# Expert stage: five row tiles instead of three between a turning and its eviction, and tokens turned one run ahead

## The chip, the cores and the metric

The kernel runs on one core of a Trainium2 chip. The metric is device time in microseconds, the median over several runs. A profile of one further execution gives the rows below; its times are microseconds from the start of the span unless marked ns. PE is TensorE, PEld its weight load, DVE VectorE, ACT ScalarE, POOL GpSimd, SP SyncE; L878 is line 878 of the kernel.

## The reference, cut to what matters

Two transformer blocks over 512 tokens of width 1024 in float32. The first has, after a mixing layer, 32 experts of which each token takes 4. The rest (retention, pooling, attention with an index, the projections) lies before and behind the stage that is changed.

```python
top_vals, top_idx = lax.top_k(logits, TOP_K)
gates = jax.nn.softmax(top_vals, axis=-1)
...
gu = lax.ragged_dot(xs, w_gu, group_sizes) + b_gu[sorted_e]
gate = jnp.minimum(gu[:, ::2], SWIGLU_LIMIT)
up = jnp.clip(gu[:, 1::2], -SWIGLU_LIMIT, SWIGLU_LIMIT)
act = (up + 1.0) * (gate * jax.nn.sigmoid(SWIGLU_ALPHA * gate))
y = lax.ragged_dot(act.astype(w_down.dtype), w_down, group_sizes) + b_down[sorted_e]
y = y * gates.reshape(-1)[order][:, None].astype(y.dtype)
out = jnp.zeros_like(xt).at[tok].add(y.astype(xt.dtype))
```

## The kernel before, in words

**Precision.** A float32 product is made of products of two parts: ScalarE copies a float32 tile to a rounded one, the high part (L877, wh), and VectorE subtracts it from the original, the low part (L878, wl). Both are needed before TensorE can finish a tile.

**Experts.** The experts are sorted by load. Wide ones have 96 slots (`CAP`), narrow ones 64 (`FEW`); `LESS[e]` says which: 0 and 1 are wide, from 2 on narrow and wide alternate, and the last, 31, is narrow too. For a wide tile TensorE makes three products for each half of 512 columns (L165 to L167), six in all. For a narrow one, high and low part of the tokens lie side by side as one stationary operand of 128 columns, so four products do (L882); the two halves of the result are then added by a "fold".

**Runs of row tiles.** Each expert has three runs of eight row tiles: `gate_up(e, 0)`, `gate_up(e, 1)` and `down(e)`. A row tile is 128 rows of a weight matrix by 1024 columns. The order is gate_up(e, 0), down(e - 1), gate_up(e, 1), and so on, so wide and narrow runs alternate. `chunks` loads two tiles by one DMA of 1024 KB on SP's queue (L145, buffers wr), splits each, multiplies, and calls `next_tile()`.

**Work between the tiles.** `later([(d, fn), ...])` hands in small steps, and `next_tile` emits a step once d more tiles have been emitted. The steps are:

- `turned` (L846): transposes the gathered tokens of the next expert, four and four (`begin`, L205), and evicts each four as a high part on ScalarE (L216) and a low part on VectorE (L217) (`end`, by `split_in`).
- `clamped` (L915), for a half of a wide expert: clamp on VectorE (L910, L911), gelu on ScalarE (L912), mul on VectorE (L913), four transposes on TensorE (L205), eviction by `split_in` to the activations a.
- `folded` (L925), for a half of a narrow one: a copy gs on ScalarE (L939), the fold on TensorE (L938), clamp, gelu, mul, and `split_in`.
- `scatter` (L943): a scaled copy ys on ScalarE (L948), and an indirect DMA on POOL's queue that adds the rows to y_d (L950).
- `table` makes the slot indices of the next experts, `gather` fetches their tokens (L837, POOL's queue), and `gated_bias` (L1027), once behind expert 10, makes the gated bias of the down-projections.

**What sets the order.** The framework orders the instructions of each engine itself, from the order in which they are emitted and from what it takes to be ready at a time; each engine then runs its own list strictly in order. PSUM tiles: three pairs of banks for products (mm), two banks for transposes and folds (tr). The split parts stand in a ring of six tiles, so ScalarE and VectorE can be at most six tiles ahead of TensorE.

Of the kernel before, what the change touches and what calls it, by code (L numbers as in the profile page):

```python
# [9 lines left out]
F32 = mybir.dt.float32  # L10
# [4 lines left out]
AF = mybir.ActivationFunctionType  # L15
ALU = mybir.AluOpType
# [4 lines left out]
NE = 32  # L21
TOPK = 4
CAP = 96
# [3 lines left out]
FEW = 64  # L27
LESS = [i >= 2 and (i % 2 == 0 or i == 31) for i in range(NE)]
NT = 4
# [91 lines left out]
class Kern:  # L121
# [10 lines left out]
    def next(self, ring):  # L132

        ring.append(ring.pop(0))
        return ring[-1]
# [75 lines left out]
        for j in range(2):  # L211
            self.split_in(self.transpose4(src, 4 * j, m=m, pool=pool), dst[j], sl)

    def split_in(self, ps, dst, sl):
        dh, dl = dst
        self.nc.scalar.activation(dh[:, :, sl], ps, AF.Copy)  # L216
        self.nc.vector.tensor_tensor(out=dl[:, :, sl], in0=ps, in1=dh[:, :, sl].bitcast(F32), op=ALU.subtract)  # L217

    def halves(self, pool, name):

# [562 lines left out]
    def moe(self, f, Q):  # L783
        tc, nc, I, c = self.tc, self.nc, self.I, self.c
        self.psum(f, "m", 3, 2)
        P = f.enter_context(tc.tile_pool(name="mp", bufs=1))
        T = f.enter_context(tc.tile_pool(name="mt", bufs=2))
# [14 lines left out]
        tabs = {}  # L802
        X = {}
        halves = [[self.wh[0].tile([128, 2, 1024], F32R, tag=tag, name=tag) for tag in ("wh", "wl")] for _ in range(2)]
        parts = [[a[:, i] for a in pair] for i in range(2) for pair in halves]
# [4 lines left out]
        def later(stages):  # L810

            self.late += [(self.at_tile + d, fn) for d, fn in stages]
# [12 lines left out]
        def tables(e, t3):  # L825
            for j in range(BATCHES[e]):
                tabs[e + j] = [a[:, j:j + 1] for a in t3]

        def table(e):

            ps = self.mm.tile([128, 2, 512], F32, tag="mm", name="mm")
            gen = self.slots_by(e, BATCHES[e], Q, ps[:, 0, :])
            later([(j, lambda: next(gen)) for j in range(BATCHES[e])] + [(BATCHES[e] + 2, lambda: tables(e, next(gen)))])
# [7 lines left out]
        def pair(m, tag):  # L841

            t = T.tile([128, 8, 2 * m], F32R, tag=tag, name=tag)
            return t[:, :, 0:m], t[:, :, m:2 * m], t

        def turned(x, m):  # L846

            p = pair(m, "x2")
            tp = {}

            def begin(j):
                tp[j] = self.transpose4(x, 4 * j, m=m)

            def end(j):
                self.split_in(tp[j], [a[:, 4 * j:4 * j + 4] for a in p[0:2]], slice(0, m))
            return p, [(1, lambda: begin(0)), (3, lambda: begin(1)), (4, lambda: end(0)), (6, lambda: end(1))]

        def turn(e):
            X[e], stages = turned(xgs[e % 2], FEW if LESS[e] else CAP)
            return stages  # L860
# [54 lines left out]
        def clamped(ps, half, p):  # L915

            gu = ps.rearrange("p a (m s) -> p (a m) s", s=2)
            gt, up = (T.tile([CAP, 512], F32, tag=tag, name=tag) for tag in ("ag", "au"))
            clamp, gelu, mul = glu(gt, up)
            tp = []  # L920
            return [(3, lambda: clamp(gu[:, :, 0], gu[:, :, 1])), (5, gelu), (6, mul),
                    (7, lambda: tp.append(self.transpose4(up, m=CAP))),
                    (10, lambda: self.split_in(tp[0], [a[:, 4 * half:4 * half + 4] for a in p[0:2]], slice(0, CAP)))]

        def folded(ps, half, p):  # L925


            gs = T.tile([128, 2, 512], F32, tag="gs", name="gs")
            v = gs.rearrange("p a (m s) -> p (a m) s", s=2)
            gt, up = (T.tile([128, 4, FEW], F32, tag=tag, name=tag) for tag in ("ag", "au"))  # L930
            clamp, gelu, mul = glu(gt, up)
            tp = []

            def fold():
                tp.append(self.tr.tile([128, 8, FEW], F32, tag="tr", name="tr"))
                for s in range(2):
                    for b in range(4):
                        nc.tensor.matmul(tp[0][:, 4 * s + b, :], v[:, b * 128:b * 128 + 128, s], c["fold"], start=True, stop=True)  # L938
            return [(3, lambda: nc.scalar.activation(gs, ps, AF.Copy)), (4, fold), (6, lambda: clamp(tp[0][:, 0:4], tp[0][:, 4:8])),  # L939
                    (7, gelu), (8, mul),  # L940
                    (9, lambda: self.split_in(up, [a[:, 4 * half:4 * half + 4] for a in p[0:2]], slice(0, FEW)))]

        def scatter(ps, gate, rows, n=1):  # L943

            self.n += 1
            m = ps.shape[0]
            y = ys[0:m, self.n % 2, :]
            nc.scalar.activation(y, ps.rearrange("p a n -> p (a n)"), AF.Copy, scale=gate[0:m])  # L948
            for o in range(0, m, m // n):
                nc.gpsimd.indirect_dma_start(out=self.y_d[:, :], out_offset=bass.IndirectOffsetOnAxis(ap=rows[0:m // n], axis=0),  # L950
                                             in_=y[o:o + m // n], in_offset=None, bounds_check=S - 1, oob_is_err=False,
                                             compute_op=ALU.add)
# [11 lines left out]
        def gate_up(e, half, raw=()):  # L964
            m = 128 if LESS[e] else CAP
            ps = self.mm.tile([m, 2, 512], F32, tag="mm", name="mm")

            def bias(n, first):
                r = FEW if LESS[e] else CAP
                nc.tensor.matmul(ps[0:r, n, :], sel[:, e:e + 1].to_broadcast([128, r]),  # L970
                                 bt[:, half * 1024 + n * 512:half * 1024 + n * 512 + 512], start=first, stop=False)
            ex = expert(e)
            chunks(lambda r, n: wgu[ex, r:r + n, half * 1024:half * 1024 + 1024], ps, X[e], raw, bias, LESS[e])
            if half == 0:
                A[e] = pair(FEW if LESS[e] else CAP, "a2")
            later((folded if LESS[e] else clamped)(ps, half, A[e]))

        def down(e):
            ps = self.mm.tile([128 if LESS[e] else CAP, 2, 512], F32, tag="mm", name="mm")
            ex = expert(e)  # L980
            chunks(lambda r, n: wdn[ex, r:r + n, :], ps, A[e], few=LESS[e])
            later([(3, lambda: scatter(ps, tabs[e][1], tabs[e][0], 2 if LESS[e] else 1))])

        def overflow():

# [41 lines left out]
        def gated_bias():  # L1027

            bd = T.tile([128, D], F32, tag="gs", name="bd")
            for r in range(0, 128, NE):  # L1030
                nc.sync.dma_start(bd[r:r + NE], I["expert_b_down"][0])
            g4 = T.tile([128, NT, 4, NE], F32, tag="ag", name="g4")
            nc.vector.tensor_copy(g4, self.G[:, :, None, :].to_broadcast([128, NT, 4, NE]))
            gT = P.tile([128, S], F32R, name="gT")
            bs = P.tile([128, D], F32R, name="bs")
            tp = self.tr.tile([128, 512], F32, tag="tr", name="tr")
            for t in range(NT):
                nc.tensor.transpose(tp[:, self.tok(t)], g4[:, t].rearrange("p a e -> p (a e)"), c["ident"])

            def parts():  # L1040
                nc.scalar.activation(gT, tp, AF.Copy)
                for r in (32, 96):
                    q = slice(r, r + NE)
                    nc.vector.tensor_tensor(out=gT[q], in0=tp[q], in1=gT[q].bitcast(F32), op=ALU.subtract)
                nc.scalar.activation(bs, bd, AF.Copy)
                nc.vector.tensor_tensor(out=bs[64:128], in0=bd[64:128], in1=bs[64:128].bitcast(F32), op=ALU.subtract)

            def products(t):
                ps = self.mm.tile([128, 2, 512], F32, tag="mm", name="mm")
                for n in range(2):  # L1050
                    nc.tensor.matmul(ps[:, n, :], gT[:, self.tok(t)], bs[:, n * 512:n * 512 + 512], start=True, stop=True)
                later([(3, lambda: nc.scalar.activation(self.h[:, t, :], ps.rearrange("p a n -> p (a n)"), AF.Copy))])
            later([(3, parts)] + [(4 + 8 * t, lambda t=t: products(t)) for t in range(NT)])

        ne = self.ne
        self.gates(self.G[:, :, 0:2], self.tcols0, 2, T)
# [18 lines left out]
        for e in range(ne):  # L1075
            if e == 0:
                table(2)
            gate_up(e, 0, raws)
            if e + 2 < ne:
                gather(e + 2)  # L1080
            if 0 < e < ne - 1:
                down(e - 1)
            if e + 1 < ne:
                later(turn(e + 1))
            if e + 3 in BATCHES:
                table(e + 3)
            gate_up(e, 1, raws)
            if e == min(10, ne - 1):
                gated_bias()
# [483 lines left out]
```

## Time and profile before

| what | us |
|---|---|
| median of 3 runs | 1867.5 |
| lowest, highest | 1863.9, 1867.83 |
| the profiled execution: its time | 1864.25 |
| the profiled execution: its span | 1862.5 |
| PE busy | 1762.6 (95%) |
| DVE busy | 1535.5 (82%) |
| ACT busy | 1186.7 (64%) |

The span goes from the first to the last instruction. Matmuls are pipelined and their ends are modelled, so a full PE is not PE at its peak. The expert stage fills the span from about 236 to 1394 us (first and last L878). "DMA share" is the mean busy share of the sixteen DMA engines.

### The profile page before, as it was taken

What the parts mean: (1) busy time and instruction counts of PE and PEld (TensorE: products, weight loads), DVE (VectorE), ACT (ScalarE), POOL (GpSimd) and SP (SyncE); (2) the same over time, 40 slices, a digit from 0 to 9 for tenths busy, and PEclk for the clock granted to TensorE, in tenths of its full rate; (3) what the DMA queues carried; (4) which work ended last, traced back from release to release, by engine and by line L of the source; (5) the groups of instructions that cost most, each with busy time, mean ns of one, the idle gap of its engine ahead of it and who ended that gap; (6) DMA issues with size and microseconds to landing.
All of it is one profiled execution on the core that took longest, in us unless ns stands there. A gap on an engine that the chain in (4) does not pass through costs nothing.

```text
span 1862.5 us, 24800 instructions
## 1 busy us (share of the span) xinstructions
PE 1762.6 (95%) x8378; PEld 1278.2 (69%) x8379; DVE 1535.5 (82%) x2637; ACT 1186.7 (64%) x1584; POOL 188.2 (10%) x120
## 2 busy tenths in 40 slices
PE   8999779899999899999999999999998999999999
PEld 6887547666666566666666666666666877787776
DVE  5574479799999789999999999999987869999542
ACT  5224258677778777777877777877875545564431
POOL 0011210121111011311110210210100000000000
PEclk9999879999999899999999999999998999999999
DMA  8225568999999999999999999999986222211211
GB/s 282 89 85 170 164 208 314 335 367 373 361 381 375 337 340 380 336 387 386 370 388 389 344 381 386 372 383 389 361 310 217 91 66 64 91 46 46 85 57 40
DMA packets 147625, 491.10 MB, mean 264 GB/s; under 512 B 14273, under 2 KB 18625, under 8 KB 147424
## 3 DMA queue, kind: packets, MB, share of 16 engines
q1 hardware_dynamic: 137600, 462.02, 66.5%
q0 software_dynamic: 8064, 22.68, 5.3%
q10 hardware_dynamic: 1824, 4.72, 0.7%
q8 instruction: 68, 1.11, 0.2%
q14 instruction: 69, 0.57, 0.1%
HBM read 470.90 MB, written 23.07 MB: 265 GB/s over the span
## 4 chain that ended last, share of the span: by engine, by line
PE 37%; DVE 18%; ACT 4%; issue 4%; DMA 1%; SPq 0%; ACTq 0%; DVEq 0%
DVE wl L878 9%; PE mm L167 8%; PE mm L166 8%; PE mm L165 8%; PE mm L882 5%; ACT wh L877 3%; PE tr L938 2%; PE tr L205 2%; PE po L1389 2%; PE tr L1472 1%; DVE isc L1335 1%; PE tr L1445 1%; DVE wl L159 1%; DVE au L913 1%; DVE m L1334 1%
## 5 line engine op out<-in xcount | busy, mean ns | idle before, releaser
L878 DVE TENSOR_TENSOR wl<-wr,wh 128x1024 fp32r<-128x1024 f32 x762 | 889.3, 1217 | 31.8 <-ACT wh L877 31.0
L877 ACT ACTIVATE wh<-wr 128x1024 fp32r<-128x1024 f32 x762 | 747.0, 1049 | 23.9 <-PE mm L166 11.2
L167 PE MATMUL mm<-wl,x 128*96 128x512 f32 x512 | 207.7, 406 | 6.2 <-DVE wl L878 5.7
L882 PE MATMUL mm<-wl,x 128*128 128x512 f32 x512 | 180.8, 434 | 28.2 <-DVE wl L878 28.0
L165 PE MATMUL mm<-wh,x 128*96 128x512 f32 x512 | 204.8, 400 | 2.5 <-ACT wh L877 2.1
L166 PE MATMUL mm<-wh,x 128*96 128x512 f32 x512 | 203.6, 398 | 0.0
L882 PE MATMUL mm<-wh,x 128*128 128x512 f32 x512 | 166.8, 397 | 0.1
L882 PEld LDWEIGHTS mm<-wl,x 128*128 128x128 f32 x512 | 81.6, 189 | 98.9 <-DVE wl L878 91.1
L950 POOL DMA_INDIRECT y_d<-ys,gi x48 | 97.8, 2037 | 438.0 <-ACT ys L948 260.4
L167 PEld LDWEIGHTS mm<-wl,x 128*96 128x96 f32 x512 | 83.5, 163 | 53.9 <-DVE wl L878 22.1
L837 POOL DMA_INDIRECT xg<-hn_d,gi x32 | 59.0, 1844 | 591.2 <-PE tr L205 540.7
L165 PE MATMUL mm<-wh,x2h 128*128 128x512 f32 (+2 forms) x288 | 115.6, 401 | 3.2 <-ACT x2h L216 3.2
L882 PEld LDWEIGHTS mm<-wh,x 128*128 128x128 f32 x512 | 96.1, 189 | 26.0 <-ACT wh L877 0.7
L166 PE MATMUL mm<-wh,x2l 128*128 128x512 f32 (+2 forms) x288 | 112.5, 391 | 0.5 <-DVE x2l L217 0.5
L167 PE MATMUL mm<-wl,x2h 128*128 128x512 f32 (+2 forms) x288 | 112.0, 390 | 0.1
L159 DVE TENSOR_TENSOR wl<-wr,wh 128x2048 fp32r<-128x2048 f32 (+3 forms) x40 | 76.4, 1915 | 38.5 <-ACT wh L158 38.3
L166 PEld LDWEIGHTS mm<-wh,x 128*96 128x96 f32 x512 | 83.8, 164 | 34.2 <-DVE x L217 0.4
L165 PEld LDWEIGHTS mm<-wh,x 128*96 128x96 f32 x512 | 83.8, 164 | 33.4 <-ACT wh L877 3.0
L167 PE MATMUL mm<-wl,a 128*96 128x512 f32 x256 | 104.4, 408 | 1.9 <-DVE wl L878 1.8
L165 PE MATMUL mm<-wh,a 128*96 128x512 f32 x256 | 101.4, 396 | 0.0
L166 PE MATMUL mm<-wh,a 128*96 128x512 f32 x256 | 101.1, 395 | 0.0
L912 ACT ACTIVATE ag<-ag 96x512 f32<-96x512 f32 (+1 forms) x64 | 33.6, 525 | 100.9 <-DVE ag L910 100.8
(438 smaller groups left out, 3134.6 us busy)
## 6 DMA issues: line engine op xcount, KB each, us to landing
wr<-in_expert_w_gate_up_dram SPq DMA_DIRECT2D x253, 1024.0 KB, 8.4
wr<-in_expert_w_down_dram SPq DMA_DIRECT2D x128, 1024.0 KB, 9.3
wr<-in_w_in_dram SPq DMA_DIRECT2D x20, 1024.0 KB, 5.0
wr<-in_w_out_dram SPq DMA_DIRECT2D x8, 1024.0 KB, 4.9
wr<-in_ple_gate_w_dram SPq DMA_DIRECT2D x4, 1024.0 KB, 9.0
wr<-in_w_in_dram SPq DMA_DIRECT2D x4, 512.0 KB, 6.9
xt<-in_x_dram POOLq DMA_DIRECT2D x8, 256.0 KB, 5.4
y_d<-h ACTq DMA_DIRECT2D x4, 512.0 KB, 3.0
```

The costliest lines, as they stand in the source:

```text
L159: nc.vector.tensor_tensor(out=lo[:, sl], in0=raw[:, sl], in1=hi[:, sl].bitcast(F32), op=ALU.subtract)
L165: mm(out, a[0], b[0], start=first, stop=False)
L166: mm(out, a[1], b[0], start=False, stop=False)
L167: mm(out, a[0], b[1], start=False, stop=last)
L205: self.nc.tensor.transpose(ps[:, j, :], src[0:m, (i0 + j) * 128:(i0 + j + 1) * 128], self.c["ident"][0:m, 0:m])
L837: nc.gpsimd.indirect_dma_start(out=xgs[e % 2][0:m], out_offset=None, in_=self.hn_d[:, :], in_offset=bass.IndirectOffsetOnAxis(ap=tabs[e][0 ...
L877: nc.scalar.activation(hi, w[:, kk], AF.Copy)
L878: nc.vector.tensor_tensor(out=lo, in0=w[:, kk], in1=hi.bitcast(F32), op=ALU.subtract)
L882: nc.tensor.matmul(ps[:, n, :], pair[2][:, k, :], part[:, n * 512:n * 512 + 512], start=k == 0 and part is hi, stop=k == 7 and part is lo)
L938: nc.tensor.matmul(tp[0][:, 4 * s + b, :], v[:, b * 128:b * 128 + 128, s], c["fold"], start=True, stop=True)
L950: nc.gpsimd.indirect_dma_start(out=self.y_d[:, :], out_offset=bass.IndirectOffsetOnAxis(ap=rows[0:m // n], axis=0), in_=y[o:o + m // n], i ...
L1389: nc.tensor.matmul(po[:, hd, :], pt[:, a * (i + 1) + k, :], v[:, k, vcol(hd)], start=(k == 0), stop=(k == i))
```

## The change

`split_in` takes a letter for the high or the low part, so that the two can be handed in as steps of their own, one tile apart. The places of the steps, in tiles behind the end of the run (or the call):

| step | before | after |
|---|---|---|
| tokens, first four: turn; high, low | 1; 4, 4 | 1; 6, 7 |
| tokens, last four: turn; high, low | 3; 6, 6 | 8; 13, 14 |
| wide half: transposes; high, low | 7; 10, 10 | 6; 11, 12 |
| narrow half: gs copy, fold, clamp, gelu, mul; high, low | 3, 4, 6, 7, 8; 9, 9 | 4, 5, 8, 9, 10; 11, 12 |
| scatter | 3 | 4 |
| gated_bias: parts, products | 3, 4 + 8t | 5, 6 + 8t |

The tokens of expert e + 1 are handed in ahead of down(e - 1) instead of behind it, thus eight tiles sooner. The gates of `gated_bias` are spread by four small copies in tiles of their own instead of one copy in a tile that the gelu's input shares.

```diff
-    def split_in(self, ps, dst, sl):
+    def split_in(self, ps, dst, sl, which="hl"):
         dh, dl = dst
-        self.nc.scalar.activation(dh[:, :, sl], ps, AF.Copy)
-        self.nc.vector.tensor_tensor(out=dl[:, :, sl], in0=ps, in1=dh[:, :, sl].bitcast(F32), op=ALU.subtract)
+        if "h" in which:
+            self.nc.scalar.activation(dh[:, :, sl], ps, AF.Copy)
+        if "l" in which:
+            self.nc.vector.tensor_tensor(out=dl[:, :, sl], in0=ps, in1=dh[:, :, sl].bitcast(F32), op=ALU.subtract)
...
-            def end(j):
-                self.split_in(tp[j], [a[:, 4 * j:4 * j + 4] for a in p[0:2]], slice(0, m))
-            return p, [(1, lambda: begin(0)), (3, lambda: begin(1)), (4, lambda: end(0)), (6, lambda: end(1))]
+            def end(j, which):
+                self.split_in(tp[j], [a[:, 4 * j:4 * j + 4] for a in p[0:2]], slice(0, m), which)
+            return p, [(1, lambda: begin(0)), (6, lambda: end(0, "h")), (7, lambda: end(0, "l")),
+                       (8, lambda: begin(1)), (13, lambda: end(1, "h")), (14, lambda: end(1, "l"))]
...
-                    (7, lambda: tp.append(self.transpose4(up, m=CAP))),
-                    (10, lambda: self.split_in(tp[0], [a[:, 4 * half:4 * half + 4] for a in p[0:2]], slice(0, CAP)))]
+                    (6, lambda: tp.append(self.transpose4(up, m=CAP))), (11, lambda: end("h")), (12, lambda: end("l"))]
...
-            return [(3, lambda: nc.scalar.activation(gs, ps, AF.Copy)), (4, fold), (6, lambda: clamp(tp[0][:, 0:4], tp[0][:, 4:8])),
-                    (7, gelu), (8, mul),
-                    (9, lambda: self.split_in(up, [a[:, 4 * half:4 * half + 4] for a in p[0:2]], slice(0, FEW)))]
+            return [(4, lambda: nc.scalar.activation(gs, ps, AF.Copy)), (5, fold), (8, lambda: clamp(tp[0][:, 0:4], tp[0][:, 4:8])),
+                    (9, gelu), (10, mul), (11, lambda: end("h")), (12, lambda: end("l"))]
...
-            later([(3, lambda: scatter(ps, tabs[e][1], tabs[e][0], 2 if LESS[e] else 1))])
+            later([(4, lambda: scatter(ps, tabs[e][1], tabs[e][0], 2 if LESS[e] else 1))])
...
-            g4 = T.tile([128, NT, 4, NE], F32, tag="ag", name="g4")
-            nc.vector.tensor_copy(g4, self.G[:, :, None, :].to_broadcast([128, NT, 4, NE]))
...
-                nc.tensor.transpose(tp[:, self.tok(t)], g4[:, t].rearrange("p a e -> p (a e)"), c["ident"])
+                g4 = T.tile([128, 4, NE], F32, tag="g4", name="g4")
+                nc.vector.tensor_copy(g4, self.G[:, t, None, :].to_broadcast([128, 4, NE]))
+                nc.tensor.transpose(tp[:, self.tok(t)], g4.rearrange("p a e -> p (a e)"), c["ident"])
...
-            later([(3, parts)] + [(4 + 8 * t, lambda t=t: products(t)) for t in range(NT)])
+            later([(5, parts)] + [(6 + 8 * t, lambda t=t: products(t)) for t in range(NT)])
...
         for e in range(ne):
             if e == 0:
                 table(2)
+                later(turn(1))
             gate_up(e, 0, raws)
             if e + 2 < ne:
                 gather(e + 2)
             if 0 < e < ne - 1:
+                later(turn(e + 1))
+            if 0 < e < ne - 1:
                 down(e - 1)
-            if e + 1 < ne:
-                later(turn(e + 1))
```

## Rows read from the trace of the kernel before

**Rows 1.** The page: busy us, share of span; DMA busy tenths in slices.
```profile
PE 1762.6 (95%) x8378; PEld 1278.2 (69%) x8379; DVE 1535.5 (82%) x2637; ACT 1186.7 (64%) x1584; POOL 188.2 (10%) x120
...
DMA  8225568999999999999999999999986222211211
```

**Rows 2.** Windows: a period, a wide run, a narrow run, two microseconds.
```profile
core 0: us, PE busy (x) PEld busy (x) DVE busy (x) ACT busy (x) POOL busy (x), PEclk, DMA share, GB/s
1195.70:1265.20 69.50, 68.02 (x305) 46.73 (x304) 64.29 (x69) 54.89 (x64) 8.75 (x5) 1.00 1.01 379
1211.90:1224.90 13.00, 13.00 (x65) 9.55 (x64) 11.58 (x14) 10.21 (x12) 0.00 (x0) 1.00 1.02 416
1224.90:1235.60 10.70, 10.58 (x47) 6.93 (x46) 10.70 (x14) 8.00 (x12) 1.44 (x1) 1.00 1.01 397
1216.00:1218.00 2.00, 2.00 (x11) 1.47 (x11) 2.00 (x3) 1.82 (x2) 0.00 (x0) 1.00 1.05 428
```

**Rows 3.** VectorE's waits from 300 to 1400: total us, times, longest.
```profile
DVE ag L910 <- PE tr L938: 31.3, 32, 4.0
DVE wl L878 <- ACT wh L877: 30.9, 59, 1.9
DVE a L217 <- ACT a L216: 14.4, 14, 1.1
DVE gi L732 <- DMA y_d<-ys,gi: 6.8, 1, 6.8
```

**Rows 4.** Timeline of VectorE in one period: start, us, instruction [idle before <-releaser].
```profile
1195.66 0.42 DVE L910 TENSOR_SCALAR ag<-tr 128x256 f32<-128x256 f32 x1 [0.89 <-PE tr L938]
...
1200.09 0.43 DVE L217 TENSOR_TENSOR a<-au,a 128x256 fp32r<-128x256 f32 x1 [1.07 <-ACT a L216]
...
1204.33 9.17 DVE L878 TENSOR_TENSOR wl<-wr,wh 128x1024 fp32r<-128x1024 f32 x8 [0.39 <-ACT wh L877]
1214.07 4.63 DVE L878 TENSOR_TENSOR wl<-wr,wh 128x1024 fp32r<-128x1024 f32 x4 [0.56 <-ACT wh L877]
1219.56 0.42 DVE L910 TENSOR_SCALAR ag<-tr 128x256 f32<-128x256 f32 x1 [0.86 <-PE tr L938]
...
1238.19 9.17 DVE L878 TENSOR_TENSOR wl<-wr,wh 128x1024 fp32r<-128x1024 f32 x8 [0.54 <-ACT wh L877]
1247.63 0.69 DVE L910 TENSOR_SCALAR ag<-mm 96x512 f32<-96x512 f32 x1 [0.27 <-PE mm L167]
...
1265.14 0.42 DVE L910 TENSOR_SCALAR ag<-tr 128x256 f32<-128x256 f32 x1 [0.90 <-PE tr L938]
```

**Rows 5.** Timeline of ScalarE in the same period.
```profile
1199.26 0.49 ACT L216 ACTIVATE x<-tr 128x384 fp32r<-128x384 f32 x1 [1.78 <-PE tr L205]
...
1226.21 0.63 ACT L912 ACTIVATE ag<-ag 96x512 f32<-96x512 f32 x1 [0.19 <-DVE ag L910]
1226.75 1.99 ACT L877 ACTIVATE wh<-wr 128x1024 fp32r<-128x1024 f32 x2
1230.67 0.49 ACT L216 ACTIVATE a<-tr 128x384 fp32r<-128x384 f32 x1 [1.93 <-PE tr L205]
1231.06 0.38 ACT L216 ACTIVATE x<-tr 128x256 fp32r<-128x256 f32 x1
1231.34 2.00 ACT L877 ACTIVATE wh<-wr 128x1024 fp32r<-128x1024 f32 x2
...
1234.20 2.00 ACT L877 ACTIVATE wh<-wr 128x1024 fp32r<-128x1024 f32 x2
1236.10 1.11 ACT L948 ACTIVATE ys<-mm,gt 128x1024 f32<-128x1024 f32 x1
```

**Rows 6.** Timeline of TensorE: the transposes behind that eviction.
```profile
1230.14 0.50 PE L205 MATMUL tr<-c_lasting,au 96*128 96x96 f32 x4
```

**Rows 7.** What SP's queue waited for, whole span: total us, times, longest.
```profile
SPq L145 <- DVE wl L878: 749.8, 324, 11.2
```

**Rows 8.** Timeline of TensorE at the hole of gated_bias.
```profile
641.84 1.22 PE L1051 MATMUL mm<-bs,gT 128*128 128x512 f32 x2 [2.10 <-DVE bs L1046]
```

More of the change, by code (lines that the diff above doesn't have):

```diff
@@ L920, in clamped, with end @@
             tp = []
+            def end(which):
+                self.split_in(tp[0], [a[:, 4 * half:4 * half + 4] for a in p[0:2]], slice(0, CAP), which)
             return [(3, lambda: clamp(gu[:, :, 0], gu[:, :, 1])), (5, gelu), (6, mul),
-                    (7, lambda: tp.append(self.transpose4(up, m=CAP))),
-                    (10, lambda: self.split_in(tp[0], [a[:, 4 * half:4 * half + 4] for a in p[0:2]], slice(0, CAP)))]
+                    (6, lambda: tp.append(self.transpose4(up, m=CAP))), (11, lambda: end("h")), (12, lambda: end("l"))]
         def folded(ps, half, p):
@@ L938, in fold, with end @@
                         nc.tensor.matmul(tp[0][:, 4 * s + b, :], v[:, b * 128:b * 128 + 128, s], c["fold"], start=True, stop=True)
-            return [(3, lambda: nc.scalar.activation(gs, ps, AF.Copy)), (4, fold), (6, lambda: clamp(tp[0][:, 0:4], tp[0][:, 4:8])),
-                    (7, gelu), (8, mul),
-                    (9, lambda: self.split_in(up, [a[:, 4 * half:4 * half + 4] for a in p[0:2]], slice(0, FEW)))]
+            def end(which):
+                self.split_in(up, [a[:, 4 * half:4 * half + 4] for a in p[0:2]], slice(0, FEW), which)
+            return [(4, lambda: nc.scalar.activation(gs, ps, AF.Copy)), (5, fold), (8, lambda: clamp(tp[0][:, 0:4], tp[0][:, 4:8])),
+                    (9, gelu), (10, mul), (11, lambda: end("h")), (12, lambda: end("l"))]
         def scatter(ps, gate, rows, n=1):
```

## Prediction

> **What bounds the kernel now.** I read the page first, for the engine shares and the slices [rows 1]: TensorE and VectorE are both near full through the expert stage, and so are the sixteen DMA engines. Three resources that full cannot be told apart from totals, so I then looked for a period. The stage repeats every 69.5 us, once for two experts, in six runs of eight row tiles: a narrow expert (64 slots, four products a tile) alternates with a wide one (96 slots, six products). The clamp behind the same fold starts at 1195.66 and again at 1265.14 [rows 4]. Some 15 such periods fill the stage; experts 0 and 1 and the last two stand outside.
>
> Cut by runs, the period has two regimes [rows 2]. In the wide run from 1211.9 TensorE is busy 13.00 us of 13.00 and VectorE only 11.58: TensorE sets the pace. In the narrow run from 1224.9 VectorE is busy 10.70 of 10.70, and the tensor engine waits for the split weights. So VectorE's idle time is paid only where it makes VectorE enter a narrow run late; in a wide run part of it is free. Over the whole period VectorE works 64.29 us, so it idles about 5.2 us. The DVE timeline says where [rows 4]: 0.89 and 0.86 at the clamp behind a fold, 1.07 at a low part waiting for the high part of the same activations, 0.39, 0.56, 0.54 (and a second 0.56 late in the period) at weight splits whose ScalarE half is late, and 0.27 at the wide clamp. That is 5.1 us. The list of VectorE's waits over the stage gives the same three sorts: fold 31.3, late wh 30.9, low part 14.4 us [rows 3].
>
> The ScalarE timeline says why its half is late [rows 5]: before each eviction of transposes it stands still for TensorE (1.78 us before the token eviction at 1199.26, 1.93 before the one at 1230.67). ScalarE had run ahead, and its in-order queue holds the next weight copies behind an eviction whose input is not there.
>
> **The written distance is not the executed one.** This decides the case. In the code the high part of a wide half stands at 10 and its gelu at 5, five tiles apart; in the trace two weight copies lie between them [rows 5]. The first token eviction of a narrow expert is written one tile behind the ys copy (4 and 3 after the same point); in the trace it precedes ys by four weight copies, thus five tiles early. The framework plans each engine's order itself: it fills what it takes for idle time with whatever is ready, so a written distance is a latest place, not a place. The transposes of au were done at 1230.14 and their eviction was next on ScalarE, the 1.93 us wait in front of it [rows 5, 6].
>
> **The change part by part.**
>
> *Tokens turned one run ahead, evictions five tiles behind.* Per expert the same eight transposes, two high and two low parts; no instruction is added. In the period, the wide tokens' evictions stand now at the seam of a wide and a narrow run, right where VectorE loses 1.07 and 0.39 us: ScalarE stood 1.78 us for those transposes, the activations' high part was queued behind, and VectorE's low part behind that [rows 4, 5]. One run earlier they leave this place. At most this gives 1.07 + 0.39 = 1.46 us a period; at least nothing, if the planner again puts each eviction right behind its transposes. The narrow tokens likewise leave the seam in front of the 0.54 us wait at 1238.19: 0 to 0.54 us. The planner has pulled forward by up to five tiles; with the same reach an eviction written two tiles later comes out up to two tiles later, and the wait goes; with a free hand it comes out as near as before. I take the middle of 0 and 2.00: 1.0 us a period.
>
> *Fold, gs copy, clamp (3, 4, 6 to 4, 5, 8).* Upper bound 0.89 + 0.86 + 2 x 0.56 = 2.87 us a period, lower bound nothing. I take nothing: these waits lie in wide runs, where TensorE is full 13.00 of 13.00 us, so VectorE coming out of the clamp earlier finds the next limit, the wide clamp, which the change leaves at 3 and where VectorE already waits 0.27 us [rows 2, 4].
>
> *High and low part one tile apart, mul and transposes both at 6, scatter at 4.* Same instructions; ys frees its PSUM tile a weight copy later at most, two runs before that tile is written again. Zero; the cover is that distance. Without it a late PSUM tile would cost TensorE about a weight split's time, once a run; I find no such wait among the longest.
>
> *Work moved.* The wide tokens' low part (0.55 us, about the length of the 96-slot forms) may leave one narrow run and enter another: zero net, at the bounds plus or minus 0.55 a period, 8 us in all.
>
> *Queues.* The gather of a next expert's tokens must land eight tiles sooner. The tight one is expert 4: its indices wait for expert 1's scatter, 6.8 us on VectorE, once [rows 3]. Its transposes come about a narrow run (10.7 us, [rows 2]) sooner; 0 to 6.8 us once, taken as 0. The buffer they free lets a later gather start sooner. SP's queue is not passed: its loads stand 749.8 us waiting for VectorE to free a raw buffer [rows 7], so faster VectorE work means earlier loads.
>
> *gated_bias.* One copy becomes four quarter copies: at most 4 x 0.42 - 0.42 = 1.3 us once, by the 128x256 clamp of [rows 4]; at least nothing. The hole there (TensorE waits 2.10 us for it, [rows 8]) comes of a chain of bias work and fold, which keeps its order: zero.
>
> **Sum.** 15 periods x 1.0 = 15 us off 1862.5 gives 1847.5; with the 1.75 us that this execution had around its span, 1849.25. Its own time, 1864.25, lies 3.25 us under the median of the runs, 1867.5, so I say 1852 for a median. Within 0.2% (3.7 us) is what a measurement here can't tell from no change.
>
> **DMA as a ceiling.** The period moves 379 GB/s x 69.5 us = 26.3 MB with a share of 1.01; in its best two microseconds 428 GB/s, which would carry it in 61.5 us [rows 2]. So the rows leave between 0 and 8 us of room a period. The list of ScalarE's waits names no load in front of a weight copy in the stage, so I take the room as enough for 1 us.
>
> The Trainium skill, "DMA: Bandwidth & Descriptors", section "Where 436 GB/s comes from", speaks against the change: a core's HBM share of about 358 GB/s binds loads from HBM, below a fabric ceiling of 435. By that the period could not be shorter than 73.5 us, an estimate from its figure, and nothing could be gained. The trace differs (379 GB/s over a period, 428 at best), so the measured numbers decide; its fabric ceiling agrees with the 428.
>
> **The rivals.**
>
> *The planner undoes it, or DMA is the wall.* The evictions are placed by readiness as before, or the queues, full at 1.01, give no more. For it: the five tiles of early placement [rows 5], the share [rows 2]. Against it: loads wait for buffers, not the reverse [rows 7]. Time: 1864 to 1871. Chance 0.22. The skill's rule above is this rival's second half.
>
> *The wait moves to a worse place (slower).* The narrow tokens' transposes now fall into a wide run that also has a fold. If their eviction lands at the seam of that run and the next narrow one, VectorE loses there 1.46 us more and enters late a narrow run in which it is busy 10.70 of 10.70; if the place it left gives nothing back, 15 x 0.39 to 15 x 1.46 us are lost: 1873 to 1889. It decides once the eviction stands less than two tiles behind its transposes, as now at 1230.67. Chance 0.22.
>
> *Five tiles hold as written.* From the whole 2.00 us of the token seams up to all 5.1 but the 0.27 go: 15 x 2.0 to 15 x 4.8, 30 to 72 us, 1795 to 1837, nearer the upper end, since the fold's share lies where TensorE is full [rows 2]. For it: all these waits are of one sort. Against: the early places [rows 5]. Chance 0.14.
>
> **How the numbers follow.** Forecast (partial gain, 4 to 30 us, 1837 to 1863) 0.42, the rivals 0.22, 0.22, 0.14. The range leaves out the better part of the large gain and the worse half of the loss, together about 0.2: 1823 to 1879. Faster by over 0.2%: 0.42 + 0.14 less the forecast's low edge, 0.55; within 0.2%: 0.21; slower: 0.24.
>
> **What would show it.** Right: in a period the low-part wait of 1.07 us and the 0.39 behind it are gone, ScalarE's 1.78 us wait for token transposes is under 0.5, the period is 68 to 69 us, and the fold waits of 0.9 and the 0.56 stay. Undone: the same waits under other start times, period 69.5. Slower: a wait of about 1 us at the seam behind the other wide run. Wrong altogether: weight copies waiting for loads, or fold waits gone. The largest doubt is how far the planner honours the written places.

## The result: slower by 0.7%

| kernel | median us | range | ratio to before, 95% interval |
|---|---|---|---|
| before (5 runs) | 1867.8 | 1863.9 to 1868.7 | |
| after (5 runs) | 1879.2 | 1878.0 to 1885.2 | 1.007 [1.0051, 1.0089] |

The change costs 11.4 us. The forecast was 1852 in a range of 1823 to 1879: the sign is wrong, and the time lies 0.2 us above the range's upper end. The profiled execution of after took 1885.17 us, the longest of the five, and that of before 1864.25, 3.6 us under its median. So the two traces lie further apart than the medians.

The page of after and the window of one period, beside [rows 1, 2]:

```profile
PE 1767.0 (94%) x8378; PEld 1277.7 (68%) x8379; DVE 1535.0 (81%) x2640; ACT 1184.9 (63%) x1584; POOL 183.8 (10%) x120
```
```profile
core 0: us, PE busy (x) PEld busy (x) DVE busy (x) ACT busy (x) POOL busy (x), PEclk, DMA share, GB/s
1212.90:1283.60 70.70, 67.84 (x305) 46.53 (x305) 64.26 (x68) 54.77 (x64) 8.78 (x5) 1.00 1.01 375
```

The work is the same: VectorE is busy 64.26 us a period (64.29 before), TensorE 67.84 (68.02), at the same granted clock of 1.00. The period is 70.70 us instead of 69.48. In these two traces, between tiles 72 and 720 of the stage's 768, VectorE's subtractions fall behind those of before by 15.9 us, evenly; 3.2 us had come earlier (the wait for gi is 8.2 us, 6.8 before), 2.7 come behind the stage and 0.8 is regained: the 20.9 us between the two spans. What grew is VectorE's idle time. Its waits from 300 to 1400 us (total, times, longest), beside [rows 3]:

```profile
DVE ag L913 <- PE tr L943: 42.1, 31, 4.0
DVE wl L881 <- ACT wh L880: 39.7, 78, 1.9
DVE gi L734 <- DMA y_d<-ys,gi: 8.2, 1, 8.2
DVE x L219 <- ACT x L217: 7.0, 25, 0.3
```

And where in the period, by VectorE's timeline (idle time and releaser in brackets), beside [rows 4]:

```profile
1212.91 0.43 DVE L913 TENSOR_SCALAR ag<-tr 128x256 f32<-128x256 f32 x1 [1.34 <-PE tr L943]
...
1216.58 0.56 DVE L219 TENSOR_TENSOR x<-tr,x 128x384 fp32r<-128x384 f32 x1 [0.31 <-ACT x L217]
1217.53 2.36 DVE L881 TENSOR_TENSOR wl<-wr,wh 128x1024 fp32r<-128x1024 f32 x2 [0.39 <-ACT wh L880]
1219.81 0.42 DVE L219 TENSOR_TENSOR a<-au,a 128x256 fp32r<-128x256 f32 x1
1220.73 9.17 DVE L881 TENSOR_TENSOR wl<-wr,wh 128x1024 fp32r<-128x1024 f32 x8 [0.50 <-ACT wh L880]
1230.46 4.63 DVE L881 TENSOR_TENSOR wl<-wr,wh 128x1024 fp32r<-128x1024 f32 x4 [0.56 <-ACT wh L880]
1236.43 0.42 DVE L913 TENSOR_SCALAR ag<-tr 128x256 f32<-128x256 f32 x1 [1.34 <-PE tr L943]
...
1240.04 0.42 DVE L219 TENSOR_TENSOR x<-tr,x 128x256 fp32r<-128x256 f32 x1 [0.25 <-ACT x L217]
1240.99 2.36 DVE L881 TENSOR_TENSOR wl<-wr,wh 128x1024 fp32r<-128x1024 f32 x2 [0.53 <-ACT wh L880]
...
1255.68 9.17 DVE L881 TENSOR_TENSOR wl<-wr,wh 128x1024 fp32r<-128x1024 f32 x8 [0.32 <-ACT wh L880]
1265.19 0.69 DVE L913 TENSOR_SCALAR ag<-mm 96x512 f32<-96x512 f32 x1 [0.35 <-PE mm L167]
```

With a second 0.55 behind the other gs copy these are 6.4 us; in [rows 4] they were 5.1. The low part that waited 1.07 us is gone, as forecast, but not by the tokens' doing (e2, e5). In its place stand 1.34 twice at the fold's clamp (0.89 and 0.86 before), and a seam that had no wait before: at 1240, between a wide run with a fold and the narrow run behind it, VectorE now stands 0.25 and 0.53 us. ScalarE's timeline says what it stood for, beside [rows 5]:

```profile
1216.06 0.49 ACT L217 ACTIVATE x<-tr 128x384 fp32r<-128x384 f32 x1 [2.27 <-PE tr L205]
...
1239.62 0.39 ACT L217 ACTIVATE x<-tr 128x256 fp32r<-128x256 f32 x1 [2.31 <-PE tr L205]
1239.90 2.00 ACT L880 ACTIVATE wh<-wr 128x1024 fp32r<-128x1024 f32 x2
```

The narrow tokens' first eviction is ScalarE's next instruction from 1237.31 on (1239.62 less 2.31), but its transposes come at 1239.13, as TensorE's timeline shows (beside [rows 6]). It is written five tiles behind them and executed right behind them. ScalarE stands 2.31 us, and the weight copies queued behind it come late.

```profile
1235.76 0.64 PE L943 MATMUL tr<-c_small,gs 128*128 128x64 f32 x4
...
1239.13 0.46 PE L205 MATMUL tr<-c_lasting,xg 64*128 64x64 f32 x4
```

SP's loads still stand for VectorE, 631.3 us (749.8 in [rows 7]), and the hole of gated_bias is 2.67 us (2.10 in [rows 8]):

```profile
SPq L145 <- DVE wl L881: 631.3, 281, 12.3
```
```profile
649.65 1.22 PE L1058 MATMUL mm<-bs,gT 128*128 128x512 f32 x2 [2.67 <-DVE bs L1053]
```

### The profile page after: what moved, and what is told of

It reads as the page before. It is cut to its first block, busy times and chain, and to the rows that moved or that the text cites. A ratio compares the mean times of both kernels' runs of the same rounds, so it can differ in the third digit from the quotient of the medians.

```text
span 1883.4 us, 24834 instructions
## 1 busy us (share of the span) xinstructions
PE 1767.0 (94%) x8378; PEld 1277.7 (68%) x8379; DVE 1535.0 (81%) x2640; ACT 1184.9 (63%) x1584; POOL 183.8 (10%) x120
## 5 line engine op out<-in xcount | busy, mean ns | idle before, releaser
L885 PE MATMUL mm<-wl,x 128*128 128x512 f32 x512 | 180.1, 433 | 31.4 <-DVE wl L881 31.3
L885 PE MATMUL mm<-wl,a 128*128 128x512 f32 x256 | 89.9, 432 | 18.3 <-DVE wl L881 16.7
```

The costliest lines, as they stand in the source:

```text
L885: nc.tensor.matmul(ps[:, n, :], pair[2][:, k, :], part[:, n * 512:n * 512 + 512], start=k == 0 and part is hi, stop=k == 7 and part is lo)
```

## The experiments

Three theories run through the expectations. **F**: the fold carries the loss (on TensorE its second half came two weight matmuls later, while the clamp kept its place among VectorE's subtractions). **T**: turning the tokens ahead carries it. **P**: the planner put the evictions back to where it takes their inputs to be ready, so the written distances never took effect.

Each time is a median of 4 to 12 runs. Ratios are to the kernel before, on the same chip, with their 95% intervals; 0.001 is 1.9 us.

### One part of the change put back

**The fold's steps back** (e1):

```diff
-            return [(4, lambda: nc.scalar.activation(gs, ps, AF.Copy)), (5, fold), (8, lambda: clamp(tp[0][:, 0:4], tp[0][:, 4:8])),
-                    (9, gelu), (10, mul), (11, lambda: end("h")), (12, lambda: end("l"))]
+            return [(3, lambda: nc.scalar.activation(gs, ps, AF.Copy)), (4, fold), (6, lambda: clamp(tp[0][:, 0:4], tp[0][:, 4:8])),
+                    (7, gelu), (8, mul), (9, lambda: end("h")), (9, lambda: end("l"))]
```

> The changed kernel with the folded steps alone put back (copy, fold, clamp at 3, 4 and 6 tiles, the rest as before). Theory F (the fold's matmuls now stand two weight matmuls later on TensorE while the clamp stays where it was on VectorE, so each of the two clamps of a period waits some 0.46 us more): 15 periods of 0.93 us come back, 14 us, and the time is about 1865. Theory T (the tokens turned one run ahead cost it): nothing comes back, 1879. If both share it, between.

Measured: 1882.8, ratio 1.0086 [1.0073, 1.0099]. Nothing came back; theory F falls. VectorE's waits show how: the fold's are as before again, and a wait for the activations' high part has come for them, at both seams where tokens stand (1.07 and 1.01 us a period).

```profile
DVE wl L881 <- ACT wh L880: 35.4, 69, 1.9
DVE ag L913 <- PE tr L943: 31.0, 32, 4.0
DVE a L219 <- ACT a L217: 27.6, 27, 1.1
```

**The tokens back** (e2):

```diff
-            if 0 < e < ne - 1:
-                later(turn(e + 1))
             if 0 < e < ne - 1:
                 down(e - 1)
+            if e + 1 < ne:
+                later(turn(e + 1))
...
-            return p, [(1, lambda: begin(0)), (6, lambda: end(0, "h")), (7, lambda: end(0, "l")),
-                       (8, lambda: begin(1)), (13, lambda: end(1, "h")), (14, lambda: end(1, "l"))]
+            return p, [(1, lambda: begin(0)), (4, lambda: end(0, "h")), (4, lambda: end(0, "l")),
+                       (3, lambda: begin(1)), (6, lambda: end(1, "h")), (6, lambda: end(1, "l"))]
```

> The changed kernel with the turning of tokens alone put back (queued behind down, stages at 1, 3, 4 and 6 tiles, high and low part together). Theory F: the old seam waits (1.07, 0.39, 0.54 us) return and the new ones leave, so within some 5 us of 1879. Theory T: the 11 us lost come back, about 1868. By the waits of the two traces, the new placement has 2.30 us of such waits a period and the old 2.00, so that about 4 us of the 11 would be T's.

Measured: 1868.8, ratio 1.0011 [1.0003, 1.002]. About ten of the 11 us are T's, though the fold's waits stay long in this kernel (42.9 us). The estimate of 4 us, a sum over the waits of the two traces, was too low: the waits at different places were not equal in what they cost. The activations' low part doesn't wait here either, though the tokens are back (14.4 us in 14 waits before):

```profile
DVE a L219 <- ACT a L217: 0.5, 1, 0.5
```

**The wide steps back** (e3):

```diff
-                    (6, lambda: tp.append(self.transpose4(up, m=CAP))), (11, lambda: end("h")), (12, lambda: end("l"))]
+                    (7, lambda: tp.append(self.transpose4(up, m=CAP))), (10, lambda: end("h")), (10, lambda: end("l"))]
```

> The changed kernel with the wide experts' steps alone put back (transposes at 7 tiles, both parts at 10). All theories: the executed order of these steps hardly moves, so 1879 within 2 us. A time under 1874 says that the wide steps carry part of the loss.

Measured: 1880.2, ratio 1.0078 [1.0065, 1.0091]: no part in it.

**Scatter and gate bias back** (e4), with one copy of the gates again:

```diff
-            later([(4, lambda: scatter(ps, tabs[e][1], tabs[e][0], 2 if LESS[e] else 1))])
+            later([(3, lambda: scatter(ps, tabs[e][1], tabs[e][0], 2 if LESS[e] else 1))])
...
-            later([(5, parts)] + [(6 + 8 * t, lambda t=t: products(t)) for t in range(NT)])
+            later([(3, parts)] + [(4 + 8 * t, lambda t=t: products(t)) for t in range(NT)])
```

> The changed kernel with the scatter's step back at 3 tiles and the gate bias stage back to one copy of all four tiles and its old places. Theories F and T: at most the 2.4 us by which the start of the experts came later (the wait for gi is 8.2 us against 6.8) and the 2.7 us more behind the experts, so 1874 to 1879. A rival, that the start and the end carry most of it: 1870 or less.

Measured: 1879.4, ratio 1.0073 [1.006, 1.0086]: no part either.

### Tokens ahead, alone and by halves

**Only the tokens' part, on the kernel before** (e5), that is, the changed kernel with the edits of e1, e3 and e4 together:

> The kernel before with one part of the change alone: the tokens turned one run ahead, at the new stages. Theory T (this part carries the loss, by the narrow tokens' evictions at the seam from a wide run that has a fold to a narrow run): a wait of about 0.25 + 0.52 us a period comes, 15 periods, 11 to 14 us, so 1878 to 1881. A rival, that it costs only together with the other parts: under 1871.

Measured: 1882.7, ratio 1.0093 [1.0077, 1.0108]. One part alone costs 17 us, just above the range expected, and no less than the whole change; the two intervals overlap. The activations' low part now waits twice a period instead of once:

```profile
DVE a L219 <- ACT a L217: 27.5, 27, 1.1
```

So that wait left the changed kernel with the later evictions of the narrow half, not with the tokens. The part itself is two things, the earlier call and the new stages; no run takes them apart.

**Narrow tokens back, wide tokens still ahead** (e9):

```diff
+            if m == FEW:
+                return p, [(1, lambda: begin(0)), (3, lambda: begin(1)), (4, lambda: end(0, "hl")), (6, lambda: end(1, "hl"))]
...
-            if 0 < e < ne - 1:
+            if 0 < e < ne - 1 and not LESS[e + 1]:
                 later(turn(e + 1))
             if 0 < e < ne - 1:
                 down(e - 1)
+            if 0 < e < ne - 1 and LESS[e + 1]:
+                later(turn(e + 1))
```

> The changed kernel with the narrow experts' tokens alone turned as before (behind down, stages 1, 3, 4, 6); the wide experts' tokens stay a run ahead. If the loss is the narrow tokens' eviction at the seam from a wide run with a fold to a narrow run (0.25 + 0.52 us a period): 11 us come back, 1868. If the wide tokens turned ahead carry it: 1879. If both: about 1874.

Measured: 1869.0, ratio 1.0018 [1.0009, 1.0027], as with all tokens back. The loss is the narrow tokens'; turning the wide ones ahead neither gains nor costs beyond the noise.

### The written places held

Each step is queued, on every engine that it uses, behind the weight work of the tile at which it is written: `self.behind` holds that tile's wh copy, wl subtraction and last matmul. This sets the order of issue only; no compute instruction is added.

```diff
+        def held(fn):
+            def go():
+                with ExitStack() as behind:
+                    for ins in self.behind:
+                        behind.enter_context(tc.issue_after(ins))
+                    fn()
+            return go
...
-            self.late += [(self.at_tile + d, fn) for d, fn in stages]
+            self.late += [(self.at_tile + d, held(fn) if self.behind else fn) for d, fn in stages]
```

**After, all steps held** (e6):

> The changed kernel, with every step of the experts queued on its engines behind the weight work of the tile at which it is written, so that five tiles do lie between a turning or fold and its eviction. Theory P (the planner moved the evictions back to where their inputs are ready, so the written distances never took effect): the fold's waits (42 us), the tokens' (7 us) and most of the 40 us behind the weights' high parts leave VectorE; 30 us or more under 1879, 1800 to 1850. A rival, that VectorE's idle time is set by its neighbours' rate and only turns up elsewhere: 1870 or more.

Measured: 1827.3, ratio 0.9797 [0.9781, 0.9813], in the range of theory P. The fold's waits left VectorE as expected (6.3 us, 42.1 in the changed kernel); those behind the weights' high parts did not (37.4 us, 39.7).

**Before, all steps held** (e7):

> The kernel before, held to its written places in the same way, so that three tiles lie between. Theory P: the fold's waits (31 us) mostly leave, as the clamp then has two narrow tiles or more behind the fold; 10 to 40 us under 1866.5. If this is as fast as the changed kernel held, three tiles are enough and five are worth nothing. The rival of neighbours' rate: 1860 or more.

Measured: 1834.1, ratio 0.9833 [0.982, 0.9847]. The time is in the range of theory P, but not for the reason written there: the fold's waits did not leave (36.5 us in all, 31.3 before). What left are waits behind the weights' high parts (18.9 us, 30.9 before) and the activations' (0.7, 14.4 before).

**After with the tokens back, all held** (e8):

> The changed kernel held to its written places, but with the tokens' turning put back behind down and its old stages. Against the changed kernel held: theory T as a matter of place (narrow tokens at a seam) says that, once held to their tiles, the tokens turned ahead are not at a seam any more, so the two agree within 5 us; if turning ahead costs wherever it lands, this one is faster by 10 us or more.

Measured: 1824.7, ratio 0.9777 [0.9763, 0.979].

Theory P holds in what it says of the order: the same instructions in another order of issue (e6) are 52 us faster than the changed kernel. That readiness is what the planner went by, these runs don't show. In e8 a period is 66.26 us (843.31 to 909.57): VectorE idles 2.1 us in it, and TensorE is busy for 65.90:

```profile
843.31:909.57 66.26, 65.90 (x305) 47.19 (x304) 64.02 (x68) 54.87 (x64) 13.34 (x5) 1.00 1.02 395
```
```profile
843.31 0.42 DVE L922 TENSOR_SCALAR ag<-tr 128x256 f32<-128x256 f32 x1 [0.69 <-PE tr L952]
864.34 5.77 DVE L889 TENSOR_TENSOR wl<-wr,wh 128x1024 fp32r<-128x1024 f32 x5 [0.52 <-ACT wh L888]
887.33 0.42 DVE L922 TENSOR_SCALAR ag<-tr 128x256 f32<-128x256 f32 x1 [0.21 <-PE tr L952]
892.18 1.23 DVE L889 TENSOR_TENSOR wl<-wr,wh 128x1024 fp32r<-128x1024 f32 x1 [0.30 <-ACT wh L888]
894.70 2.36 DVE L889 TENSOR_TENSOR wl<-wr,wh 128x1024 fp32r<-128x1024 f32 x2 [0.39 <-ACT wh L888]
909.57 0.42 DVE L922 TENSOR_SCALAR ag<-tr 128x256 f32<-128x256 f32 x1 [0.70 <-PE tr L952]
```

Held, three tiles (e7) give 32 us and five (e6, e8) 38 to 41, so the two more tiles, with the rest of the change, are worth 7 to 9 us where they exist. Held, tokens ahead (e6) cost 2.5 us against tokens behind (e8), not 10, and the two intervals overlap.

### One sort of step held

The changed kernel with `held` on the steps of one sort, the rest left to the planner: the tokens (e10), the narrow products (e11), the wide products (e12). For e11:

```diff
-            later((folded if LESS[e] else clamped)(ps, half, A[e]))
+            stages = (folded if LESS[e] else clamped)(ps, half, A[e])
+            later([(d, held(fn)) for d, fn in stages] if LESS[e] else stages)
```

> The changed kernel with the steps of the tokens alone held to the tiles at which they are written; all else is left to the planner. If the place of the eviction is what costs: the waits at both seams (0.25 + 0.52 and 0.31 + 0.39 us a period) leave, 12 to 22 us under 1879, so 1857 to 1868. If turning ahead costs wherever it lands: 1875 or more.

Measured: 1871.3, ratio 1.0027 [1.0018, 1.0036], between the two answers: 8 us come back, though not the 12 that the first answer wanted. The seam is free, but the fold's waits grew to 59.0 us.

> The changed kernel with the narrow experts' products alone held to their tiles (copy at 4, fold at 5, clamp at 8, and on). If the 52 us that holding everything gave came from the fold's waits (42 us on VectorE, 1.34 us twice a period): 1837 to 1850. If they came from the steps together, as each early eviction only hands its wait to the next: 1860 or more.

Measured: 1875.2, ratio 1.0052 [1.004, 1.0064]. It is the second answer, steps that hand their waits on; the 4 us under the changed kernel (1.0051 to 1.0089) are not clear of noise. The fold's wait more than halved (18.5 us, 42.1); 2.32 us stand at the wide clamp instead, and 2.85 behind a late weight copy:

```profile
871.32 0.42 DVE L922 TENSOR_SCALAR ag<-tr 128x256 f32<-128x256 f32 x1 [0.70 <-PE tr L952]
875.53 0.69 DVE L922 TENSOR_SCALAR ag<-mm 96x512 f32<-96x512 f32 x1 [2.32 <-PE mm L167]
...
924.91 2.48 DVE L889 TENSOR_TENSOR wl<-wr,wh 128x1024 fp32r<-128x1024 f32 x2 [2.85 <-ACT wh L888]
```

> The changed kernel with the wide experts' products alone held to their tiles (clamp at 3, transposes at 6, evictions at 11 and 12). The traces show no wait of over 0.34 us a period at the wide clamp and none at their evictions, so by the fold's theory 1872 to 1879; by the theory of steps together up to 20 us less.

Measured: 1880.8, ratio 1.0075 [1.0062, 1.0089]: nothing, as the fold's theory had it within 2 us.

One by one these are 8, 4 and -1.5 us, of which only the 8 are clear of noise; together with the scatter's copy, the tables and the gate bias they are 52. Two more kernels ask whether a free step takes the waits over, or the scatter's copy carries the gain: **all products held, tokens free** (e13), and **products and tokens held, the scatter and the rest free** (e14). In e13 the `if LESS[e]` of e11 is dropped; e14 holds the steps of `turned` as well.

> The changed kernel with the products of narrow and wide experts held to their tiles; tokens, the scatter's copy and the rest are left to the planner. If a free step takes over the waits of the held ones (in the run with the narrow products alone held, the fold's wait halved and a wait of 2.32 us stood at the wide clamp instead): holding both is worth far more than 4 us plus nothing, 1835 to 1860. If the scatter's copy carries the gain: 1870 or more.

Measured: 1889.6, ratio 1.013 [1.0115, 1.0146]. By the number it falls to the second answer, but the trace gives little of its reason: ScalarE waits 32.5 us at the scatter's copy, and 118.6 at the tokens' evictions (63.2 in the changed kernel). Held products make the kernel 10 us slower as long as the tokens are free. The tokens' steps take the waits over, and more: 2.50 us and 0.52 behind it at one place of the period; 2.85 at another.

```profile
882.91 0.42 DVE L219 TENSOR_TENSOR x<-tr,x 128x256 fp32r<-128x256 f32 x1 [2.50 <-ACT x L217]
883.86 1.23 DVE L889 TENSOR_TENSOR wl<-wr,wh 128x1024 fp32r<-128x1024 f32 x1 [0.52 <-ACT wh L888]
...
931.47 2.48 DVE L889 TENSOR_TENSOR wl<-wr,wh 128x1024 fp32r<-128x1024 f32 x2 [2.85 <-ACT wh L888]
```

> The changed kernel with products and tokens held; only the scatter's copy, the tables and the gate bias are left to the planner. If free steps take over waits and the scatter's copy, on ScalarE, is one of several: 1827 to 1840. If the scatter's copy carries the gain: 1860 or more. If it matters nothing: 1827.

Measured: 1842.3, ratio 0.9862 [0.9845, 0.9878], just over the first answer's upper end and far from the second. Holding the tokens too turns 1889.6 into 1842.3; the scatter's copy, the tables and the gate bias are the last 15 us to 1827.3. ScalarE's waits in e14 name the copy: 44.9 and 31.1 us for its two kinds of products.

```profile
ACT ys L965 <- PE mm L167: 44.9, 14, 3.3
ACT ys L965 <- PE mm L894: 31.1, 15, 3.2
```

### What still waits in the held kernel

Two versions of e8: the fold's steps alone (e16), or those and the tokens' (e15).

```diff
-            return [(4, lambda: nc.scalar.activation(gs, ps, AF.Copy)), (5, fold), (8, lambda: clamp(tp[0][:, 0:4], tp[0][:, 4:8])),
-                    (9, gelu), (10, mul), (11, lambda: end("h")), (12, lambda: end("l"))]
+            return [(4, lambda: nc.scalar.activation(gs, ps, AF.Copy)), (4, fold), (8, lambda: clamp(tp[0][:, 0:4], tp[0][:, 4:8])),
+                    (10, gelu), (11, mul), (12, lambda: end("h")), (12, lambda: end("l"))]
```

> The held kernel with tokens turned behind down, changed where it still waits: the fold one tile earlier (4), gelu and product one later (10, 11), evictions of the tokens later (begin 1 and 4, high part 5 and 8, low part 6 and 9). Its VectorE still idles 2.1 us a period (0.21 and 0.70 at the fold's clamps, 0.52, 0.30, 0.39 behind the weights' high parts). If distances set the waits, most of that leaves: 15 to 30 us under 1824.7, 1795 to 1810. If the weights' DMA (394 GB/s in a period now) is the next wall: 1818 to 1826.

Measured: 1822.9, ratio 0.9766 [0.9745, 0.9786], in the range of the second answer. That range also holds 1824.7, the time of e8, so it would fit a change worth nothing and doesn't show loads to be the wall.

> The same with the fold's steps alone changed (copy 4, fold 4, clamp 8, gelu 10, product 11, parts 12), the tokens as in the held kernel. By the waits of that kernel the two waits at the fold's clamp (0.21 and 0.70 us a period) leave: 14 us under 1824.7, 1811. If the DMA is the next wall: 1818 to 1826.

Measured: 1820.75, ratio 0.9755 [0.974, 0.9769], the lowest median of all: 45 us under before. The waits behind the fold are no longer among VectorE's longest (11.5 us in e8), but only 4 of the 14 us came, and the intervals of e8, e15 and e16 overlap. In the traces the expert stage got no shorter: the subtractions start at 236.81 us in both, and the last group ends at 1349.91 in e8 and at 1350.03 in e16.

```profile
1345.28 4.63 DVE L889 TENSOR_TENSOR wl<-wr,wh 128x1024 fp32r<-128x1024 f32 x4 [0.39 <-ACT wh L888]
```
```profile
1345.40 4.63 DVE L889 TENSOR_TENSOR wl<-wr,wh 128x1024 fp32r<-128x1024 f32 x4
```

What else limits the stage was there in e8 already. TensorE is busy 65.78 of 66.00 us here, 65.90 of 66.26 there. ScalarE waits for the experts' weights, which its list of before doesn't name at all, 45.7 us here and 42.3 there (e8 first, then e16):

```profile
ACT wh L888 <- DMA wr<-in_expert_w_down_dram: 21.4, 28, 2.0
ACT wh L888 <- DMA wr<-in_expert_w_gate_up_dram: 20.9, 27, 3.0
```
```profile
ACT wh L888 <- DMA wr<-in_expert_w_gate_up_dram: 26.6, 35, 5.2
...
ACT wh L888 <- DMA wr<-in_expert_w_down_dram: 19.1, 26, 1.9
```
```profile
840.00:906.00 66.00, 65.78 (x306) 47.25 (x305) 63.34 (x68) 54.17 (x64) 13.05 (x5) 1.00 1.03 393
```

Which of the two binds, no run shows.

## Why the prediction was wrong

**The step that failed is the first one, the tokens turned ahead.** It was costed at a gain of 1.0 us a period, between 0 and 2.00. The planner was rightly said to place evictions early, but the lower bound taken from that was "nothing", as if the new place could be no worse than the old. Measured, the step alone costs 17 us on the kernel before (e5) and about 10 of the 11 us in the change (e2): 0.7 to 1.1 us a period over 15 periods. The half about the wide tokens is nothing (e9). Its 1.07 us were put down to the tokens and are not theirs: the wait stays with the tokens alone ahead (e5), comes back with the fold's old steps (e1), and is gone with the tokens back (e2). That it left as forecast is luck. The 0.39 stayed, and ScalarE's wait for the tokens' transposes, which should have fallen from 1.78 us to under 0.5, is 2.27.

"One run earlier they leave this place" fails by the change's own table. The second four tokens are turned at 8 behind a call that comes eight tiles sooner, instead of at 3: three tiles sooner, and one tile ahead of where the first four were turned. In the trace they stand where the first four stood, ahead of the same weight copy (1216.06 here, 1199.26 in [rows 5]); only the first four left. The half about the narrow tokens, counted as a gain of up to 0.54, is the loss.

**It is the rival "the wait moves to a worse place", at the place that it named:** the transposes fall into a wide run that also has a fold, the eviction lands at the seam to the next narrow run right behind them (ScalarE's 2.31 us), and VectorE loses 0.25 + 0.53 us there, then enters a narrow run late. It was priced at 0.39 to 1.46 us a period; the period grew by 1.22, though the medians' 11.4 us are only 0.76 for each of 15. By VectorE's list alone more of it stands at the fold's clamps (0.93) than at the seam (0.78); it is the runs e1, e2 and e9 that put the loss at the tokens.

**The fold at nothing: right**, for part of the reason given. Its waits, which were to stay, grew from 31.3 to 42.1 us, yet putting it back gains nothing, since the time goes to the next wait (e1). That is not the wide clamp, as the prediction had it (5.5 us in e1), but the activations' low part (27.6).

**High and low part apart, mul, scatter; gated_bias: right**, at nothing each (e3, e4). **Gather: right in its bounds**, 8.2 us against 6.8, once.

**DMA as a ceiling:** the slower period moved 375 GB/s and didn't put the room to the test. The held kernels show that there is some: they reach 393 to 395 GB/s over 66 us, and there loads are among the waits. The Trainium skill's "DMA: Bandwidth & Descriptors", section "Where 436 GB/s comes from", gives a core about 358 GB/s, its half of a stack's 716, and says that this binds loads from HBM. For this kernel, on one core, the measured rate is 10% above that over whole periods, so the measurement decides.

**"Five tiles hold as written"** was given 1795 to 1837, against the evidence of the early places. The change does not do it; held by force, the same steps do, at 1827 (e6), inside that range. But three tiles held give 32 of these 38 us (e7): most of it is the holding, and going from three tiles to five is worth 7 to 9 us. What the diff lacks is a means to enforce its places.

**Why one step held gains so little** is shown in part. In this kernel the ring of six split tiles lets ScalarE and VectorE run ahead of TensorE. A step whose input comes from TensorE and that is issued early makes ScalarE or VectorE give up that lead; where the first such step no longer waits, the next one does (e1, e11, e13). Only with all of them late does the lead stay (e6 to e8). That the planner reckons TensorE to be further along than it is would explain the early places; this was only argued, from the order of the executed lists. Open as well is why e13 is slower than the changed kernel, and not only no faster.

**Two readings** were a little off, without weight in the sum. The transposes of au at 1230.14 begin there and are done at 1230.64; their eviction follows at 1230.67. And 69.5 us is the period's shortest form: of fourteen stretches of 48 tiles in the trace of before, six last 70.9 to 77.6 us.

## What to carry to other kernels

A distance written in the source is a request. Before costing a change of distances, count in the trace how many weight tiles lie between producer and eviction on the evicting engine, and if they are fewer than written, tie the order of issue itself. Do it for every step that waits for the lagging engine at once: one tied step hands its wait to the next, and can even lose. Put a wait down to a step only when a run with that step alone moves it. And a move that is "at worst nothing" has a new neighbour; price the wait there before giving the old one as a gain.

## What the runs showed of the hardware

Nothing about a unit by itself was a surprise. The three limits lie closer than the profile of before suggested: a period of 69.5 us with TensorE at 68.02 and VectorE at 64.29 us came down to 66.26 in e8, with TensorE busy 65.90 for the same 305 matmuls, so part of the 68.02 us was not needed: a busy time with modelled ends is no floor. The sixteen DMA engines showed a share of 1.01 at 375 GB/s and 1.03 at 393: the share was full in both, and only the bytes moved told that there was room.
